# Recurrent stage with its factors two units ahead, its gated outputs spread over the next units, and the prompt's operands asked for at its end

## The chip, the cores and the metric

The kernel runs on one core of one Trainium2 chip. The metric is device time in microseconds (us) of one execution: 2415.64 us, the median of 3 runs (2414.82 to 2417.95). The engines are TensorE (PE; its weight loads are PEld), VectorE (DVE), ScalarE (ACT), GpSimd (POOL) and SyncE (SP), whose queue issues nearly all loads and stores (SPq).

## The reference

One inference step of a hybrid layer for a prompt of 2048 tokens and 8 samples of 4 tokens. One RMSNorm and one combined input projection (1024 to 5912 columns) feed two branches:

- native sparse attention: compressed, top-8 selected and window branches over 8 heads, with gates;
- HGRN2, a gated linear recurrence, 4 heads of 128 by 128 state;

both are gated, projected, merged through sigmoid gates (ma, mb), projected once more, added to the input and normalised. The recurrence is the part at issue:

```python
def step(S, xs):
    qc, kc, vc, gc = xs
    G = jnp.cumsum(gc, axis=2)
    o_inter = jnp.einsum('bhtd,bhde->bhte', qc * jnp.exp(G), S)
    D = jnp.where(tri, G[:, :, :, None, :] - G[:, :, None, :, :], -jnp.inf)
    A = jnp.einsum('bhtd,bhtsd,bhsd->bhts', qc, jnp.exp(D), kc)
    o = o_inter + jnp.einsum('bhts,bhse->bhte', A, vc)
    S = jnp.exp(Gl)[..., None] * S + jnp.einsum('bhsd,bhse->bhde', kc * jnp.exp(Gl[:, :, None, :] - G), vc)
...
o = o * lax.rsqrt(jnp.mean(o * o, axis=-1, keepdims=True) + EPS)
return o.reshape(B, T, B_WIDTH) * norm_g * jax.nn.silu(zB), S
```

## The kernel before

The kernel is one program whose stages are written as Python generators. `along(steps, ns)` runs a stage: after each `yield` it calls `fill(ns)`, which emits input projection matmuls worth about ns nanoseconds. A projection matmul multiplies float16 pairs (high and low parts), three products of 8 by 128x128 for each block of up to 512 tokens: 24 matmuls into one accumulator `ps` (two of them, `fps`). The groups of columns come in a fixed order (q, f, qb, ib, zb, z, ma, mb); the last, mb ("gate", L424), goes in pieces of 512 or 272 tokens, each through ScalarE into one of 3 buffers (`row`, later `piece`) and by a store (mb_d, L441) to memory.

The code gives only a priority. A scheduler puts every engine's instructions into one fixed order, by this priority and by its own estimate of what is ready. The engines then run their orders strictly, waiting on one another by semaphores.

The recurrent stage, `hgrn()` (L620), handles **units**: a chunk of 256 tokens and one of 4 heads, 32 units in all; the four heads of a chunk are a **group** here. Of a unit:

- `factors` loads the unit's operands and makes the decayed factors: a scan G and the subtractions on VectorE (five X, L728), exponentials on ScalarE, products on GpSimd (L731, L732, L693 to L703).
- `scores` transposes Kd (L739) and makes the two 128x128 score blocks out of small matmuls (L751, L755); VectorE masks them into AT (own, L762 to L765).
- `values` multiplies with v and with the state S (pu L774, ov L778 and L780), updates S on VectorE (L785), and ScalarE copies o and sums its squares into `ss` (L790, L793).

One unit's factors are made while the unit before goes through `values`. After the fourth head of a chunk, `rsqrt` makes the reciprocal root by a Newton chain of 16 small VectorE instructions (L649, L237 to L244, L651), and `gate_out` is emitted for the four heads in a row: VectorE scales o (L656), TensorE transposes it (L659), VectorE multiplies by zt (L662), and the halves gh, gl are stored to obh_d, obl_d. Beside the units, from the seventh on, `sample_heads` handles the 4 heads of the samples step by step; its state update multiplies kd with v masked for 4 samples at a time (vm on VectorE, L836; product L838).

Behind the stage comes `attention_setup` (it loads szs and stores oah_d, oal_d, L1409 to L1414), then `prompt_phase`: `open_block` loads the queries of the first blocks (L1500 to L1503), `want` the window keys (L1480 to L1485), `load_keys` the rest (L1359 to L1365); `prep` makes the compressed scores (L1567 to L1607) of two blocks with `pfill` between its steps; then the attention runs block by block, with what is left of the mb pieces and the output projections (L1777) between its tiles.

Of the kernel before, what the change touches and what calls it, by code (L numbers as in the profile page):

```python
# [10 lines left out]
F32 = mybir.dt.float32  # L11
F32R = mybir.dt.float32r
F16 = mybir.dt.float16
# [8 lines left out]
NP = 2048  # L22
# [109 lines left out]
def trunk_kernel(ctx: ExitStack, tc: tile.TileContext, A, O):  # L132
# [487 lines left out]
    def hgrn():  # L620
        with ExitStack() as st:
# [4 lines left out]
            lmf = hc.tile([128, 8, 32], F32, name="lmf")  # L626
            sy.dma_start(lmf, A["c_lmask"].rearrange("p (l t) -> p l t", l=8))
            lmi = hc.tile([128, 8, 32], I32, name="lmi")
            ve.tensor_copy(lmi, lmf)
# [17 lines left out]
            def rsqrt(ss):  # L647
                n = ss.shape[0]
                ve.tensor_scalar(ss, ss, 1.0 / 128, EPS, op0=OP.mult, op1=OP.add)  # L649
                y = newton_rsqrt(ss, hp)  # L650
                ve.tensor_scalar(y, y, sob[:n], None, op0=OP.mult)  # L651
                return y

            def gate_out(o_sb, zt, y, nt, r, h, t0):

                ve.tensor_tensor(o_sb[:r, :nt], o_sb[:r, :nt], y[:r, :nt, None].to_broadcast([r, nt, 128]), op=OP.mult)  # L656
                pt = po.tile([128, 512], F32, name="ov")
# [12 lines left out]
            def common(h, t0, n, L):  # L670
# [24 lines left out]
                Xo = new("Xo")  # L695
# [5 lines left out]
                Kd = new("Kd", bufs=1)  # L701
                ac.activation(Kd, E2, AF.Exp)
                gp.tensor_mul(Kd, Kd, kt)  # L703
                eG = hp.tile([128, 8], F32, name="eG" + sfx)[:, :n // L]
# [10 lines left out]
            def factors(c, h):  # L715
                t0 = c * NC
                G, qt, kt, Bq, Bk, Xo, Kd, eG = common(h, t0, NC, 128)
                v = hp.tile([128, NJ, 128], F32, name="v")
# [17 lines left out]
            def scores(u):  # L736
# [6 lines left out]
                for j in range(NJ):  # L743
# [18 lines left out]
                    ve.tensor_mul(own, near[:, 3], lmf[:, 3])  # L762
# [7 lines left out]
            def values(u, ss):  # L770
# [20 lines left out]
                for j in range(NJ):  # L791
                    jk = hp.tile([128, 128], BF, name="jk")
                    ac.activation(jk, ov[:, j], AF.Square, accum_out=ss[:, h * NJ + j:h * NJ + j + 1])  # L793
# [4 lines left out]
            def sample_heads():  # L798
                for h in range(4):
# [4 lines left out]
                    sy.dma_start(S0, A["state_hgrn"][0, :, h].rearrange("b d e -> d b e"))  # L804
                    pb = po.tile([128, 512], F32, name="pk")
                    mm(pb[:32, :32], Bk, Bq, True, True)
                    AT = hp.tile([32, 32], F32, name="ATs")
                    ve.tensor_mul(AT, pb[:32, :32], lmf[:32, 3])
# [13 lines left out]
                    jk = hp.tile([32, 128], BF, name="jk_s")  # L822
                    ac.activation(jk, pt[:32, :128], AF.Square, accum_out=ss)
                    y = rsqrt(ss)
                    yield
                    gate_out(o_sb, load_z(h, 2048, 32), y, 1, 32, h, 2048)
                    pk = po.tile([128, 512], F32, name="pk").rearrange("p (a b) -> p a b", a=4)
                    pe.transpose(pk[:32, 0], Kd, ident)
                    kd = hp.tile([32, 128], F32, name="kd_s")
# [3 lines left out]
                    for b2 in range(2):  # L833
                        vm = hp.tile([32, 4, 128], F32, name="vm", bufs=1)
                        for b in range(4):
                            ve.tensor_scalar(vm[:, b], v, bd[:, 4 * b2 + b:4 * b2 + b + 1], None, op0=OP.mult)  # L836
                        pu = po.tile([128, 512], F32, name="pu").rearrange("p (a b) -> p a b", a=4)
                        mm(pu, kd, vm, True, True)  # L838
                        for b in range(4):
                            bb = 4 * b2 + b  # L840
                            ve.scalar_tensor_tensor(Sn[:, bb], S0[:, bb], eG[:, bb:bb + 1], pu[:, b], op0=OP.mult, op1=OP.add)
                    sy.dma_start(O["s_hgrn"][0, :, h].rearrange("b d e -> d b e"), Sn)

            beside = sample_heads()
            units = [(c, h) for c in range(NP // NC) for h in range(4)]
            ahead = [factors(*units[0])]
            yield
            yield from scores(ahead[0])
            outs = []
            for k, (c, h) in enumerate(units):  # L850
# [3 lines left out]
                u = ahead.pop(0)  # L854
                if k + 1 < len(units):
                    ahead.append(factors(*units[k + 1]))
                    yield
                    yield from scores(ahead[0])
# [7 lines left out]
                if h == 3:  # L866
                    y = rsqrt(ss)
                    for h2 in range(4):
                        gate_out(*outs[h2], y[:, h2 * NJ:(h2 + 1) * NJ], NJ, 128, h2, c * NC)
                        yield  # L870
# [476 lines left out]
    def attention_setup(st, a):  # L1347

        pc_ = st.enter_context(tc.tile_pool(name="pc", bufs=1, side="right"))
        KA, KB, V = a["KA"], a["KB"], a["V"]  # L1350
        a["sel0"] = pc_.tile([128, 16, 32], F32, name="h_sel0")
        for g in range(2):
            KA["s", g] = pc_.tile([100, NP], F16, name=f"kas{g}")
            KB["s", g] = pc_.tile([128, NP], F16, name=f"kbs{g}")
        V["s"] = pc_.tile([128, 16, 2, 129], F16, name="vs16")

        def load_keys(t0, t1):
            if t0 == 0:
                sy.dma_start(a["sel0"], A["c_sel0"].rearrange("p (t j) -> p t j", j=32))  # L1359
# [60 lines left out]
    def prompt_phase(a, st, pfill, state, sw):  # L1420
        KA, KB, V, TB, TQ = a["KA"], a["KB"], a["V"], a["TB"], a["TQ"]
        pu = st.enter_context(tc.tile_pool(name="pu", bufs=2, side="right"))
        pst = st.enter_context(tc.tile_pool(name="pst", bufs=2, space=PSUM, side="right"))
        pmx = st.enter_context(tc.tile_pool(name="pmx", bufs=3, space=PSUM, side="right"))
# [197 lines left out]

        state["env"]["tp"] = lambda: pmx.tile([128, 4, 128], F32, name="mx").rearrange("p a b -> p (a b)")
        wc = sw.enter_context(tc.tile_pool(name="wc", bufs=3))
        state["env"]["piece"] = lambda: wc.tile([128, 512], F32, name="piece")
        for i in range(2):
            open_block(i)
            if i == 0:
                want(ORDER[0])
                a["load_keys"](0, 512)  # L1630
            else:
                a["load_keys"](512, NP)
# [346 lines left out]
        return main  # L1979

    with ExitStack() as s2:
# [22 lines left out]
        along(hgrn(), 1250.0)  # L2004
        fill(0, ("z", 2))
        fill(350.0)
        along(attention_setup(s2, att), 15000.0)
        fill(0, ("ma", 6))
        sb.close()
        prompt_phase(att, s2, fill, state, sw)()  # L2010
# [31 lines left out]
```

## Time and profile before

| what | value |
|---|---|
| median of 3 runs | 2415.64 us |
| profiled execution | 2413.94 us |
| its span | 2412.2 us |
| mean granted TensorE clock | 0.98 |
| TensorE busy | 2279.5 us, 94% |
| VectorE busy | 1533.5 us, 64% |
| ScalarE / GpSimd busy | 1182.3 us / 1021.4 us |
| recurrent stage, first transposes to last gated product | 638 to 1323 us |

TensorE's busy time is the sum of stretches in which a matmul is recorded; what it lacks to the span are gaps. A clock under 1.00 in a stretch says that for a part of it the granted clock was the lower of its two levels (1.2 instead of 2.4 GHz). An idle time in brackets names the instruction that ended the wait.

### The profile page before, as it was taken

Reading aid. Unit: us, or ns where it says so; the run is one execution under the profiler, and the core shown is the slowest. Engines: PE = TensorE matmul, PEld = TensorE weight load, DVE = VectorE, ACT = ScalarE, POOL = GpSimd, SP = SyncE. Lnnn points to the kernel's source line nnn. Section 1 sums busy time; section 2 is a strip of 40 time slices with the busy share of each in tenths; the row PEclk is TensorE's granted clock in tenths of the full one; section 3 lists DMA queues with packets and bytes.
Section 4 is the critical chain, followed back from the end, with each engine's and each line's share of the span. In section 5 each row is a group of like instructions: output and inputs, shape, how many; then the busy total and the mean of one; then the engine's idle time right before and its main releaser. Section 6 shows DMA issues by size and latency. Waiting matters only on the chain.

```text
span 2412.2 us, 56868 instructions
## 1 busy us (share of the span) xinstructions
PE 2279.5 (94%) x22181; PEld 1545.1 (64%) x22181; DVE 1533.5 (64%) x4088; ACT 1182.3 (49%) x2606; POOL 1021.4 (42%) x1184
## 2 busy tenths in 40 slices
PE   6999998999899998999989799899999999999998
PEld 5898775555685555556656456667677666665765
DVE  7555554756613689777774356768677677767543
ACT  5544332521422266555663256356556566667663
POOL 0000102242500056555550035356656567777764
PEclk9999999999999999999999899999999999999999
DMA  6643313676842443333332533432222221211121
GB/s 205 178 127 117 127 71 107 230 257 219 256 125 75 152 142 112 115 111 116 117 102 93 141 121 95 111 85 80 63 85 83 61 63 43 72 50 48 52 58 43
DMA packets 276109, 271.89 MB, mean 113 GB/s; under 512 B 102296, under 2 KB 246176, under 8 KB 268416
## 3 DMA queue, kind: packets, MB, share of 16 engines
q1 hardware_dynamic: 267328, 230.51, 31.2%
q0 software_dynamic: 8512, 37.75, 4.7%
q8 instruction: 174, 2.85, 0.5%
q14 instruction: 95, 0.78, 0.1%
HBM read 184.66 MB, written 87.74 MB: 113 GB/s over the span
## 4 chain that ended last, share of the span: by engine, by line
PE 72%; DVE 11%; DMA 6%; ACT 4%; issue 3%; SPq 2%; POOL 1%; ACTq 0%; POOLq 0%; DVEq 0%
PE ps L375 17%; PE ps L1809 7%; PE ps L1777 7%; PE ps L456 7%; PE ps L435 5%; PE st L1666 3%; PE st L1656 3%; PE mx L1536 3%; PE ph L969 2%; DVE X L728 2%; PE po L1461 2%; PE po L1462 2%; PE po L1464 2%; DMA wraw<-in_w_in_dram 1%; PE pt L952 1%
## 5 line engine op out<-in xcount | busy, mean ns | idle before, releaser
L1455 POOL TENSOR_TENSOR Pl<-P,Ph 128x512 f16<-128x512 f32 x444 | 522.1, 1186 | 316.6 <-ACT Ph L1454 178.6
L1453 ACT ACTIVATE P<-st 128x512 f32<-128x512 f32 x444 | 264.8, 597 | 239.8 <-PE st L1666 185.3
L375 PEld LDWEIGHTS <-wh 128*128 128x128 f16 x2240 | 216.0, 98 | 167.8 <-issue 16.2
L1454 ACT ACTIVATE Ph<-st 128x512 f16<-128x512 f32 x444 | 263.1, 595 | 10.5 <-PE po L1462 8.3
L375 PE MATMUL ps<-xh,wh 128*128 128x512 f16 (+1 forms) x1120 | 229.6, 342 | 4.7 <-DVE row L388 3.5
L375 PE MATMUL ps<-xh,wl 128*128 128x512 f16 (+1 forms) x1120 | 232.9, 343 | 0.0
L375 PE MATMUL ps<-xl,wh 128*128 128x512 f16 (+1 forms) x1120 | 231.7, 341 | 0.5 <-issue 0.5
L1539 DVE TENSOR_REDUCE mps<-mx 128x1 f32<-128x512 f32 (+3 forms) x320 | 185.8, 602 | 60.3 <-PE mx L1538 29.5
L456 PE MATMUL ps<-wh,xh 128*128 128x256 f16 (+1 forms) x680 | 190.3, 280 | 10.1 <-ACT to L464 4.8
L456 PE MATMUL ps<-wh,xl 128*128 128x256 f16 (+1 forms) x680 | 189.2, 279 | 4.1 <-DVE xl L341 4.1
L456 PE MATMUL ps<-wl,xh 128*128 128x256 f16 (+1 forms) x680 | 189.9, 279 | 0.0
L1461 PEld LDWEIGHTS <-Ph 128*128 128x128 f16 x1776 | 139.8, 98 | 39.5 <-ACT Ph L1454 5.2
L375 PEld LDWEIGHTS <-wl 128*128 128x128 f16 x1120 | 109.4, 99 | 83.1 <-issue 6.1
L456 PEld LDWEIGHTS <-xh 128*128 128x128 f16 x1360 | 131.1, 99 | 32.4 <-issue 7.7
L1462 PEld LDWEIGHTS <-Ph 128*128 128x128 f16 x1776 | 128.4, 97 | 32.6 <-issue 0.5
L697 POOL TENSOR_TENSOR Xo<-Xo,qt 128x256 f32<-128x256 f32 x32 | 33.3, 1041 | 260.7 <-ACT Xo L696 210.0
L1539 DVE TENSOR_REDUCE mpw<-mx 128x1 f32<-128x512 f32 (+3 forms) x224 | 102.8, 482 | 40.5 <-PE mx L1538 40.0
L1777 PEld LDWEIGHTS <-xh 128*128 128x128 f16 x1280 | 105.0, 98 | 32.7 <-issue 7.1
L731 POOL TENSOR_TENSOR X<-X,kt 128x128 f32<-128x128 f32 x160 | 91.5, 574 | 65.4 <-ACT X L730 63.0
L1464 PEld LDWEIGHTS <-Pl 128*128 128x128 f16 x1776 | 94.2, 97 | 25.9 <-POOL Pl L1455 8.8
L1461 PE MATMUL po<-vs,Ph 128*128 128x65 f16 x1088 | 105.5, 192 | 2.6 <-DVE otmp L1553 2.0
L1462 PE MATMUL po<-vs,Ph 128*128 128x64 f16 x1088 | 104.8, 193 | 0.0
(528 smaller groups left out, 5824.0 us busy)
## 6 DMA issues: line engine op xcount, KB each, us to landing
wraw<-in_w_in_dram SPq DMA_DIRECT2D x22, 1024.0 KB
xt<-in_x_prompt_dram SPq DMA_DIRECT2D x32, 512.0 KB
ma_d<-row SPq DMA_DIRECT2D x8, 1040.0 KB
out_y_prompt_dram<-xt SPq DMA_DIRECT2D x16, 512.0 KB
sg<-ma_d SPq DMA_DIRECT2D x56, 128.0 KB
sg<-mb_d SPq DMA_DIRECT2D x56, 128.0 KB
q_d<-row SPq DMA_DIRECT2D x4, 1040.0 KB
lf_d<-row SPq DMA_DIRECT2D x4, 1040.0 KB
```

The source lines that it names most:

```text
L375: mm(ps, l[:, kc], xs(r, t0, n)[:, kc], k == 0, k == 23)
L435: mm(ps, l[:, kc, a * 128:(a + 1) * 128], xs(r, t0, n)[:, kc], k == 0, k == 23)
L456: mm(ps, x, w[:, kc], k == 0, k == 23)
L1453: ac.activation(P[:n], ps, AF.Exp, scale=1.0 / QS)
L1454: ac.activation(ph[:n], ps, AF.Exp, scale=1.0 / QS)
L1455: sub.tensor_sub(pl[:n], P[:n], ph[:n])
L1461: mm(po[:, r, :w], ph[:n, rs[r]], v[:n, :w], first and r == 0, False)
L1462: mm(po[:, r, :64], ph[:n, rs[r]], v[:n, w:w + 64], False, False)
L1464: mm(po[:, r, :w], pl[:n, rs[r]], v[:n, :w], False, last)
L1539: ve.tensor_reduce(mp_[:, r, c:c + 1], pmf[:, :n], axis=AX.X, op=OP.max)
L1777: mm(X["ps"], w[:, kc, cs], os_[o][:, kc], k == 0, k == 11)
L1809: mm(X["ps"], X["y"][y][:, kc, i0:i0 + r], W["o", kc // 4][w][:, kc % 4, cs], k == 0, k == 23)
```

## The change

1. `factors` runs two units ahead, not one; Kd, v, Xo and eG get one more buffer, jk one less, and the mask constant is loaded into a borrowed tile, of which only a 32-column part is kept (lm3).
2. Scaling (`gate_scale`) is split off `gate_out`. The four gated outputs of a chunk wait in a list `ready`; each of the next four units asks for one scale at its start and emits one `gate_out` before its values.
3. `sample_heads` makes its masks (`masked`) a step ahead of the product that reads them, and takes one step more a head.
4. `fill` after a step of the stage is asked for 1200, not 1250 ns.
5. `prompt_phase` is a generator too. Its first part, the loads of block 0 and its window keys, is emitted at the end of the recurrent stage, before `attention_setup`; the tiles of the keys are made later, in `load_keys`.

```diff
@@ -623,10 +623,12 @@
...
-            lmf = hc.tile([128, 8, 32], F32, name="lmf")
-            sy.dma_start(lmf, A["c_lmask"].rearrange("p (l t) -> p l t", l=8))
+            lm = hp.tile([128, 256], F32, name="X0").rearrange("p (l t) -> p l t", l=8)
+            sy.dma_start(lm, A["c_lmask"].rearrange("p (l t) -> p l t", l=8))
...
-            ve.tensor_copy(lmi, lmf)
+            ve.tensor_copy(lmi, lm)
+            lm3 = hc.tile([128, 32], F32, name="lm3")
+            ve.tensor_copy(lm3, lm[:, 3])
@@ -647,13 +649,15 @@
...
-                y = newton_rsqrt(ss, hp)
-                ve.tensor_scalar(y, y, sob[:n], None, op0=OP.mult)
+                y = hp.tile([128, 8], F32, name="rsy", bufs=3)[:n, :ss.shape[1]]
+                ve.tensor_scalar(y, newton_rsqrt(ss, hp), sob[:n], None, op0=OP.mult)
...
-            def gate_out(o_sb, zt, y, nt, r, h, t0):
+            def gate_scale(o_sb, y, nt, r):
...
+
+            def gate_out(o_sb, zt, nt, r, h, t0):
@@ -692,16 +696,16 @@
...
-                Xo = new("Xo")
+                Xo = new("Xo", bufs=3)
...
-                Kd = new("Kd", bufs=1)
+                Kd = new("Kd")
...
-                eG = hp.tile([128, 8], F32, name="eG" + sfx)[:, :n // L]
+                eG = hp.tile([128, 8], F32, name="eG" + sfx, bufs=3)[:, :n // L]
@@ -715,7 +719,7 @@
...
-                v = hp.tile([128, NJ, 128], F32, name="v")
+                v = hp.tile([128, NJ, 128], F32, name="v", bufs=3)
@@ -759,7 +763,7 @@
...
-                    ve.tensor_mul(own, near[:, 3], lmf[:, 3])
+                    ve.tensor_mul(own, near[:, 3], lm3)
@@ -789,7 +793,7 @@
...
-                    jk = hp.tile([128, 128], BF, name="jk")
+                    jk = hp.tile([128, 128], BF, name="jk", bufs=1)
@@ -802,10 +806,17 @@
...
+                    vm = hp.tile([32, 4, 128], F32, name="vm", bufs=1)
+
+                    def masked(b2):
+                        for b in range(4):
+                            ve.tensor_scalar(vm[:, b], v, bd[:, 4 * b2 + b:4 * b2 + b + 1], None, op0=OP.mult)
+
+                    masked(0)
...
-                    ve.tensor_mul(AT, pb[:32, :32], lmf[:32, 3])
+                    ve.tensor_mul(AT, pb[:32, :32], lm3[:32])
@@ -819,43 +830,64 @@
...
-                    jk = hp.tile([32, 128], BF, name="jk_s")
+                    jk = hp.tile([128, 128], BF, name="jk", bufs=1)[:32]
...
-                    y = rsqrt(ss)
+                    gate_scale(o_sb, rsqrt(ss), 1, 32)
...
-                    gate_out(o_sb, load_z(h, 2048, 32), y, 1, 32, h, 2048)
+                    gate_out(o_sb, load_z(h, 2048, 32), 1, 32, h, 2048)
...
-                    kd = hp.tile([32, 128], F32, name="kd_s")
+                    kd = hp.tile([32, 128], F32, name="kd_s", bufs=1)
...
-                        vm = hp.tile([32, 4, 128], F32, name="vm", bufs=1)
-                        for b in range(4):
-                            ve.tensor_scalar(vm[:, b], v, bd[:, 4 * b2 + b:4 * b2 + b + 1], None, op0=OP.mult)
...
+                        if b2 == 0:
+                            masked(1)
...
+                        if b2 == 0:
+                            yield
...
+
...
+            for _ in range(3):
+                yield
+            ahead.append(factors(*units[1]))
...
-            outs = []
+            outs, ready = [], []
+
+            def gated(step):
+
+                if ready:
+                    o_sb, zt, y, h2, c2 = ready[0]
+                    if step == 0:
+                        gate_scale(o_sb, y, NJ, 128)
+                    else:
+                        gate_out(o_sb, zt, NJ, 128, h2, c2 * NC)
+                        ready.pop(0)
+
...
+                gated(0)
+                if k + 2 < len(units):
+                    ahead.append(factors(*units[k + 2]))
+                    yield
...
-                    ahead.append(factors(*units[k + 1]))
+                    yield from scores(ahead[0])
+                if ready:
+                    gated(1)
...
-                    yield from scores(ahead[0])
@@ -865,9 +897,13 @@
...
-                    for h2 in range(4):
-                        gate_out(*outs[h2], y[:, h2 * NJ:(h2 + 1) * NJ], NJ, 128, h2, c * NC)
-                        yield
+                    ready = [(*outs[h2], y[:, h2 * NJ:(h2 + 1) * NJ], h2, c) for h2 in range(4)]
+            while ready:
+                gated(0)
+                yield
+                next(beside, None)
+                gated(1)
+                yield
@@ -1346,16 +1382,16 @@
...
-        pc_ = st.enter_context(tc.tile_pool(name="pc", bufs=1, side="right"))
...
-        a["sel0"] = pc_.tile([128, 16, 32], F32, name="h_sel0")
-        for g in range(2):
-            KA["s", g] = pc_.tile([100, NP], F16, name=f"kas{g}")
-            KB["s", g] = pc_.tile([128, NP], F16, name=f"kbs{g}")
-        V["s"] = pc_.tile([128, 16, 2, 129], F16, name="vs16")
...
+                pc_ = st.enter_context(tc.tile_pool(name="pc", bufs=1, side="right"))
+                a["sel0"] = pc_.tile([128, 16, 32], F32, name="h_sel0")
+                for g in range(2):
+                    KA["s", g] = pc_.tile([100, NP], F16, name=f"kas{g}")
+                    KB["s", g] = pc_.tile([128, NP], F16, name=f"kbs{g}")
+                V["s"] = pc_.tile([128, 16, 2, 129], F16, name="vs16")
@@ -1420,8 +1456,6 @@
...
-        pst = st.enter_context(tc.tile_pool(name="pst", bufs=2, space=PSUM, side="right"))
-        pmx = st.enter_context(tc.tile_pool(name="pmx", bufs=3, space=PSUM, side="right"))
@@ -1620,15 +1654,19 @@
...
+        open_block(0)
+        want(ORDER[0])
+        yield
+        pst = st.enter_context(tc.tile_pool(name="pst", bufs=2, space=PSUM, side="right"))
+        pmx = st.enter_context(tc.tile_pool(name="pmx", bufs=3, space=PSUM, side="right"))
...
-            open_block(i)
...
-                want(ORDER[0])
...
+                open_block(1)
@@ -1976,7 +2014,7 @@
...
-        return main
+        main()
@@ -2001,13 +2039,16 @@
...
-        along(hgrn(), 1250.0)
+        along(hgrn(), 1200.0)
...
+        prompt = prompt_phase(att, s2, fill, state, sw)
+        next(prompt)
...
-        prompt_phase(att, s2, fill, state, sw)()
+        for _ in prompt:
+            pass
...

```

The scheduler turns this into new orders on all engines. Three places follow, before and after.

VectorE, first group of four units, from the start of the Newton chain (ss is the sum of squares, rsq and rsz are the chain's values). Before:

```order
L649 TENSOR_SCALAR ss<-ss 128x8
L237 TENSOR_SCALAR rsq<-ss 128x8
L685 SCALAR_TENSOR_TENSOR G<-rst,lf 128x256
L238 TENSOR_TENSOR rsq<-magic,rsq 128x8
L688 TENSOR_TENSOR E<-G 128x256
L700 TENSOR_TENSOR E<-G 128x256
L241 TENSOR_TENSOR rsz<-rsq 128x8
L242 TENSOR_TENSOR rsz<-rsz,ss 128x8
L243 TENSOR_SCALAR rsz<-rsz 128x8
L244 TENSOR_TENSOR rsq<-rsq,rsz 128x8
```

After:

```order
L651 TENSOR_SCALAR ss<-ss 128x8
L692 TENSOR_TENSOR E<-G 128x256
L237 TENSOR_SCALAR rsq<-ss 128x8
L732 TENSOR_TENSOR X_9881<-G 128x256
L732 TENSOR_TENSOR X_9887<-G 128x256
L732 TENSOR_TENSOR X_9893<-G 128x256
L766 TENSOR_TENSOR own<-p_9724,lm_8646 128x32
L238 TENSOR_TENSOR rsq<-magic,rsq 128x8
L732 TENSOR_TENSOR X_9899<-G 128x256
L732 TENSOR_TENSOR X_9905<-G 128x256
L766 TENSOR_TENSOR own<-p_9759,lm_8646 128x32
```

The chain's rows stood nearly next to each other; now the X and own rows of later units stand between them.

SyncE, end of the recurrent stage: gh and gl are its last gated output, szs and OSh, OSl belong to `attention_setup`, qs, qc, qb are the queries of block 0. Before:

```order
L667 DMA obh_d<-gh 128x256
L668 DMA obl_d<-gl 128x256
L441 DMA mb_d<-piece 128x272
L1409 DMA szs<-sz_d 64x8x32
L1359 DMA h_sel_16055<-in_c_sel_dram 128x512
L1361 DMA kas_16056<-ksx_d_89 64x512
L1362 DMA kbs_16057<-ksx_d_89 128x512
L1364 DMA kas_16056<-in_c_kblk_dram 36x2048
L1413 DMA oah_d<-OSh 64x8x32
L1414 DMA oal_d<-OSl 64x8x32
L1361 DMA kas_16058<-ksx_d_90 64x512
L1362 DMA kbs_16059<-ksx_d_90 128x512
```

After:

```order
L671 DMA obh_d<-gh 128x256
L672 DMA obl_d<-gl 128x256
L441 DMA mb_d<-row 128x272
L1534 DMA qs<-qh_d 64x4x128
L1534 DMA qc<-qh_d 64x4x128
L1534 DMA qb<-qh_d 64x4x128
L1535 DMA qc<-tc_d_87 32x512
L1537 DMA qb<-ql_d 64x4x128
L1534 DMA qs<-qh_d 64x4x128
L1534 DMA qc<-qh_d 64x4x128
L1534 DMA qb<-qh_d 64x4x128
L1535 DMA qc<-tc_d_88 32x512
```

The loads of block 0 stood behind szs and the stores of OSh and OSl; now they follow the last store of the recurrent stage, and szs stands behind all 24 of them and three stores of pieces.

TensorE, first two blocks of the prompt's preparation: xd carries the maxima, st are compressed scores, Ph their probabilities, ps and wh a piece of the mb projection. Before:

```order
L1445 MATMUL mx<-h_id,xd_16447 128x128
L1576 LDWEIGHTS kac_6516
L1576 MATMUL st<-qc,kac_6516 128x512
L1576 LDWEIGHTS kac_6525
L1576 MATMUL st<-qc,kac_6525 128x512
L1461 LDWEIGHTS Ph
L1461 MATMUL mx<-vc,Ph 128x97
L1462 LDWEIGHTS Ph
```

After:

```order
L435 MATMUL ps<-xh_124,wh 128x272
L1610 LDWEIGHTS kac_6516
L1610 MATMUL st<-qc,kac_6516 128x512
L435 LDWEIGHTS wh
L435 MATMUL ps<-xl_128,wh 128x272
L1610 LDWEIGHTS kac_6525
L1610 MATMUL st<-qc,kac_6525 128x512
L435 LDWEIGHTS wh
```

Between the second score product and the first probability product stood nothing; now 27 projection matmuls follow the second score product before the first probability product, and one stands between the two.

## Rows read from the trace of the kernel before

**Rows 1.** The page's busy line: us, share of the span, instructions.

```profile
PE 2279.5 (94%) x22181; PEld 1545.1 (64%) x22181; DVE 1533.5 (64%) x4088; ACT 1182.3 (49%) x2606; POOL 1021.4 (42%) x1184
```

**Rows 2.** Stretches: length, busy us of PE, PEld, DVE, ACT, POOL, clock, DMA.

```profile
864.00:990.00 126.00, 115.38 (x1240) 72.54 (x1239) 113.33 (x316) 78.88 (x266) 80.45 (x130) 0.96 0.37 122
990.00:1294.00 304.00, 287.32 (x2919) 181.50 (x2916) 214.87 (x657) 166.90 (x577) 146.82 (x246) 0.98 0.34 108
1294.00:1324.00 30.00, 30.00 (x152) 14.99 (x150) 14.95 (x57) 8.17 (x15) 0.00 (x0) 1.00 0.31 100
1324.00:1400.00 76.00, 62.29 (x391) 35.01 (x390) 29.49 (x101) 17.41 (x27) 5.45 (x9) 0.87 0.50 141
1500.00:1600.00 100.00, 89.56 (x1069) 64.44 (x1067) 74.42 (x252) 46.67 (x92) 47.56 (x56) 0.95 0.41 108
900.00:950.00 50.00, 42.56 (x515) 27.92 (x514) 47.00 (x147) 30.46 (x110) 35.09 (x58) 0.90 0.30 93
1150.00:1200.00 50.00, 48.29 (x564) 31.79 (x563) 39.08 (x118) 33.43 (x116) 29.74 (x47) 1.00 0.43 137
```

**Rows 3.** TensorE in order of time, recurrent stage: start, us, what [idle before].

```profile
935.11 0.66 PE L659 MATMUL ov<-ident,o_sb 128*128 128x128 f32 x2 [4.94 <-DVE o_sb L656]
...
985.73 1.09 PE L838 MATMUL pu<-vm,kd_s 32*128 32x512 f32 x2 [2.29 <-DVE own L764]
...
1051.68 1.09 PE L838 MATMUL pu<-vm,kd_s 32*128 32x512 f32 x2 [3.42 <-DVE vm L836]
...
1264.61 0.69 PE L659 MATMUL ov<-ident,o_sb 128*128 128x128 f32 x2 [4.99 <-DVE o_sb L656]
```

**Rows 4.** Chain of waits, 1290 to 1420: start, us, what.

```profile
1326.88 2.47 DMA szs<-sz_d
...
1331.06 2.24 DMA oal_d<-OSl
1333.36 0.60 SPq L1500
...
1349.47 3.45 DMA mb_d<-piece
...
1371.61 1.17 POOL Pl L1455
...
1404.38 5.18 PE ps L435 x24
```

**Rows 5.** TensorE in order of time, prompt's preparation and first output product.

```profile
1353.75 1.87 PE L435 MATMUL ps<-xh,wh 128*128 128x512 f16 x4 [3.35 <-ACT piece L440]
...
1379.37 0.45 PE L1603 MATMUL mx<-ident,repp 128*128 128x128 f32 x1 [2.68 <-DVE repp L1599]
...
1519.03 0.47 PE L1603 MATMUL mx<-ident,repp 128*128 128x128 f32 x1 [3.12 <-DVE repp L1599]
1522.42 0.27 PE L1777 MATMUL ps<-oah,xh 128*128 128x32 f16 x4 [2.92 <-DMA oah<-oah_d]
```

**Rows 6.** VectorE in order of time, second group: start and scaling of the chain.

```profile
926.60 0.43 DVE L649 TENSOR_SCALAR ss<-ss 128x8 f32<-128x8 f32 x1
...
934.54 0.76 DVE L656 TENSOR_TENSOR o_sb<-o_sb,rsq 128x256 f32<-128x256 f32 x2
```

**Rows 7.** TensorE in order of time, start of the recurrent stage.

```profile
638.27 0.44 PE L739 MATMUL pk<-ident,Kd 128*128 128x128 f32 x2 [3.08 <-POOL Kd L703]
...
642.20 0.69 PE L751 MATMUL p<-X 128*64 128x64 f32 x4 [3.49 <-POOL X L732]
...
851.56 0.62 PE L780 MATMUL ov<-S,Xo 128*128 128x128 f32 x2 [2.26 <-DVE S L783]
```

**Rows 8.** Tile X, 870 to 1290: ns min/median/max, first and last start.

```profile
L728 DVE TENSOR_TENSOR X<-G x125: 396/417/959, 873.8 to 1257.6; 128x256 f32<-128x256 f32 x125
...
L731 POOL TENSOR_TENSOR X<-X,kt x125: 442/458/2510, 878.7 to 1263.4; 128x128 f32<-128x128 f32 x125
```

**Rows 9.** Groups by line, VectorE, 864 to 1294: busy us, mean ns, idle.

```profile
L728 DVE TENSOR_TENSOR X<-G 128x256 f32<-128x256 f32 x125 | 68.6, 603 | 0.0
```

## The prediction

> **What bounds the kernel now.** I read the page's busy line first, then stretches, then the waits inside them, then the chain of waits. TensorE is busy 94% of the span [rows 1], so only two things can shorten it: gaps between its matmuls and half-clock time. The stretches [rows 2] show where these are. I count as lost, in each, the time without matmuls plus (1 − granted clock) × length.
>
> - 864 to 990, the middle of the recurrent stage (units 4 to 11, from unit 3's state update to unit 11's): 10.6 + 5.0 = 15.7 us lost, VectorE busy 113.3 of 126 us, 90%.
> - 990 to 1294 (units 12 to 31): 16.7 + 6.1 = 22.8 lost, VectorE 71%.
> - 1294 to 1324, the stage's tail: nothing.
> - 1324 to 1400, the prompt phase's preparation: 13.7 + 9.9 = 23.6 lost.
> - 1500 to 1600: 10.4 + 5 = 15.4 lost.
>
> The waits behind these numbers [rows 3]: twice some 5 us for a gated product whose scaling VectorE had not done (935, 1264), 3.4 and 2.3 us at the sample update. At 1324 to 1354 the chain [rows 4] leaves the engines for SyncE's queue: the sample's szs load, its store behind VectorE, then the loads of block 0 one by one from 1333 on, and behind them the store of a finished gate piece, without which ScalarE had no buffer and TensorE stood 3.35 us [rows 5]. Then come the short steps of the preparation with nothing between them, up to the 2.68 us at 1379.
>
> **The change, part by part.** Work on TensorE is the same, but for where projection matmuls stand. I count them in sets of 24 of 512 columns; one takes 5.18 us [rows 4].
>
> *Less projection inside the stage.* From unit 3 to 11 there were 14.1 sets, now 12.9 (6.4 us less); from 11 to 31 37.7, now 31.5 (32.3 us less). They are run later, so this gains nothing: the same stretches with the loss they have now, but the new sets, would take 126 − 6.4 = 119.6 and 304 − 32.3 = 271.7 us. Free of loss they are 103.9 and 248.9.
>
> *VectorE does not shrink with them.* Between the same state updates it has 312 instructions before and 308 now, then 657 and 652 (two of the 2 us weight passes fewer, about 5 us). So it needs 113 us where TensorE needs 104, and 210 where TensorE needs 249. In units 4 to 11 VectorE is the bound: at its 90% of today they take 126 us, a loss of 22 where it is 15.7; at 97%, 117 us, a loss of 13. The first is as likely as the second, so I take 17. For units 12 to 31 VectorE's share rises from 71% to about 82%. Spreading removes the places where its work came in a heap, so the loss may fall to 7 us (2 to 3%), or stay at 8%, 20 us. I take 13. Together 30 against 38.5: 8 us gained, between 4 us lost and 18 gained.
>
> *Gated outputs, one per unit.* The scale is asked for a unit ahead, but the order shows that all four scales still stand together behind the reciprocal root. What moved is the root's chain: between its first row and the scales stood 27, 29, 29, 27, 25, 26, 35, 16 rows in the eight groups, now 45, 37, 34, 51, 37, 49, 31, 16. The first product stands about as far behind its unit as before (9 to 12 us of matmuls, now 9.5 to 14). In the second group the chain took 926.6 to 934.5, 8 us, and TensorE waited 4.94 [rows 3, 6]. So I count the first product of a group as a wait that stays and only the second to fourth as free; this is in the 17 and 13.
>
> *Masks a step ahead.* At 1051 the sample's second update product waited 3.42 us for its masks, at 985 the first 2.29 us. With the masks made a step earlier both waits, 5.7 us [rows 3], should go; they are part of the 8 us.
>
> *Two units ahead, at the start.* The projection matmuls in front of the first transposes are the same, so the 3.08 and 3.49 us at 638 and 642 and the 2.26 at 851 [rows 7] stay: 0. The further buffers, the moved mask constant and the shared scratch tile cost one small VectorE copy, under 1 us, early in the stage, where the clock and TensorE wait for loads.
>
> *Prompt operands at the stage's end.* The 24 loads stand now in front of szs and its stores. They still wait for the stage's last store, since they take its memory. At 0.6 us each [rows 4] they hold SyncE 14 us, and the piece stores behind them wait so long. TensorE has 5.7 sets, 29 us, between the last gated product and the first compressed logits (it had 3.0, 15.5 us). Three piece buffers and two accumulators hold some 21 us of them (two pieces of 272 columns, three of 512); the queue is free again after 14 us and a landing before and behind of 2.2 us each, as the store of the chain took, 19 in all: the 3.35 us should go, with little to spare. The preparation now has 2 to 6 us of projection between its steps, against links of up to 1.17 us [rows 4], so most of its waits go; the last selection step still has none (2.68 us stays). Of 23.6 us lost I keep 8: 15 to 16 gained, at least 0, at most 20.
>
> *Block 0's first output product* at 1519 [rows 5]: the selection wait (3.12) and the load (2.92) have the same neighbours now. I take 0, with 4 us either way.
>
> The sum against the profiled execution, 2413.9 us (span 2412.2 and 1.7 around it): 8 + 15.5 = 24 us less, 2390. The median shown is 1.7 above that execution, so **2392**. Its own range is 2380 to 2404, the middle part of both terms' ends (2 to 16 and 10 to 20 us gained).
>
> **A rule that speaks against it.** The subtraction that makes X on VectorE reads two operands in SBUF and takes 396 ns at the least and 959 at the most; GpSimd's product beside it takes 442 to 2510 [rows 8]. The Trainium skill (SBUF — State Buffer, "Who interferes with whom") says that a VectorE instruction with two SBUF inputs and a GpSimd instruction that reads SBUF take turns at one port pair, the later one blocked for the whole instruction. The spread in the rows agrees with that, and by the rule a stage in which both are denser would slow both. It is the last rival.
>
> **Rivals.**
> 1. *The recurrent waits go altogether.* With factors two units ahead VectorE could run at 97% in units 4 to 11, and the products of a group could all come after their scales: loss 13 + 4, so 21 us gained, and 20 at the boundary: 2374. For it: 1150 to 1200 lost only 1.7 us with VectorE at 78% [rows 2]. Against it: VectorE needs more than TensorE in units 4 to 11.
> 2. *The boundary keeps its wait.* SyncE's block is only moved ahead; if the release comes later or the loads take longer, the gate pieces run out of buffers at another place and the preparation is late. Gain 4 to 8 in the stage, 0 here: 2410.
> 3. *Slower: the root's chain sets the pace.* The eight chains have 300 rows instead of 214; 86 rows at VectorE's 0.35 us (328 us for 973 rows, [rows 2]) are 30 us, and the product waits for each if VectorE is full. After the wait of 4.94 us the granted clock was 0.90 over 900 to 950 [rows 2], its lower level for a part: 5 us more; three such add 15. Less masks 6 and boundary 15: 24 us slower, 2440. It decides once each of the seven long chains costs over 3 us more wait.
> 4. *Slower by the port.* If each of 125 subtractions took the longest 959 ns instead of the mean 603 [rows 8, 9], VectorE would need 45 us more; 372 us at 90% are 414 for both stretches, where 391 holds today's loss: 23 slower, less 15: 2424.
>
> **Chances.** Forecast 0.50, rival 1 0.20, rival 2 0.16, rival 3 0.09, rival 4 0.05. The range reaches from just under rival 1 to rival 2 and the near part of rivals 3 and 4: 2372 to 2420. A difference within 0.2% (4.8 us) can't be told from none. The forecast is faster but for 0.02 beyond its own range, rival 1 wholly, rival 2 in 0.07 of its 0.16, else the same; rivals 3 and 4 are slower but for 0.02: faster 0.75, same 0.13, slower 0.12.
>
> **What would show it.** Right: units 4 to 11 with VectorE at 90% or more and TensorE's loss still near 17; no sample-update wait over 1 us; the first product of a group waiting more than the other three; the chain at the stage's end without SyncE, no wait for a piece, and one selection wait near 3 us. Wrong: the boundary's 24 us still lost, or half-clock stretches at most groups. My sum fails if the recurrent stage gains over 20 us or loses any.

## The result and the profile after

The changed kernel takes 2393.57 us (median of 4 runs, 2388.3 to 2394.5), the kernel before beside it 2416.8 (4 runs): ratio 0.9891, 95% interval 0.9871 to 0.9911. That is 23 us faster by the medians and 26 by the ratio. A second measurement, on a later occasion, gave 0.9904 (0.9890 to 0.9918). The profiled execution has a span of 2392.4 us against 2412.2.

The busy line of the page answers to [rows 1]; below it are stretches between the same points of the program as in [rows 2] (length, then busy us of PE, PEld, DVE, ACT and POOL, clock, DMA share, GB/s):

```profile
PE 2276.5 (95%) x22181; PEld 1543.9 (65%) x22181; DVE 1523.3 (64%) x4089; ACT 1180.8 (49%) x2606; POOL 1018.8 (43%) x1184
```

```profile
865.00:984.00 119.00, 110.31 (x1164) 69.78 (x1162) 112.33 (x313) 77.00 (x263) 78.64 (x129) 0.94 0.39 125
984.00:1250.00 266.00, 257.67 (x2773) 163.38 (x2774) 198.17 (x657) 159.80 (x573) 146.69 (x245) 0.99 0.36 113
...
1274.00:1304.00 30.00, 30.00 (x173) 16.82 (x172) 7.99 (x35) 6.63 (x9) 0.82 (x5) 1.00 0.43 115
1304.00:1404.00 100.00, 94.64 (x691) 54.48 (x690) 46.54 (x132) 35.78 (x57) 18.54 (x16) 0.97 0.45 132
1404.00:1504.00 100.00, 90.22 (x985) 62.63 (x984) 63.69 (x204) 60.15 (x103) 48.55 (x48) 0.96 0.40 112
1504.00:1604.00 100.00, 95.81 (x1138) 67.58 (x1137) 73.99 (x242) 46.08 (x96) 49.56 (x57) 0.99 0.33 87
```

Units 4 to 11 are the first row, 12 to 31 the second, the first compressed logits come at 1304. The recurrent units take 385 us instead of 430, and lose 8.7 + 7.1 = 16 and 8.3 + 2.7 = 11 us; before it was 15.7 and 22.8. VectorE is busy 94% of the first row, 74% of the second. Behind 1304 the first 100 us lose 9 us; before, the first 100 us behind the first logits (at 1339) lost 24.

TensorE's longest waits there, singly (start, us, what, idle before and what ended it), answer to [rows 3, 5]:

```profile
927.55 0.40 PE L822 MATMUL pu<-ATs,vs__10316 32*128 32x32 f32 x2 [3.03 <-DVE S L789]
...
998.71 0.69 PE L663 MATMUL ov<-ident,o_sb 128*128 128x128 f32 x2 [3.41 <-DVE o_sb L658]
...
1110.61 0.44 PE L663 MATMUL ov<-ident,o_sb 128*128 128x128 f32 x2 [1.99 <-DVE o_sb L658]
...
1356.10 0.45 PE L1637 MATMUL mx<-ident,repp 128*128 128x128 f32 x1 [3.29 <-DVE repp L1633]
...
1499.27 0.48 PE L1637 MATMUL mx<-ident,repp 128*128 128x128 f32 x1 [5.26 <-DVE repp L1633]
```

The waits for masks are gone; those for a scaled output fell from 10.7 to 5.7 us, the two long ones each the first of its group. The new wait at 927 is one of VectorE's own order. VectorE in order of time there:

```profile
924.38 0.50 DVE L397 SCALAR_TENSOR_TENSOR row<-ps,neg,row 128x272 f32<-128x272 f32 x1
924.92 2.32 DVE L207 TENSOR_REDUCE trk<-row 128x1 f32<-128x2080 f32 x1
927.16 0.34 DVE L789 SCALAR_TENSOR_TENSOR S<-S,eG,pu 128x128 f32<-128x128 f32 x1
```

A state update of 0.34 us, for which TensorE waits, stands behind a maximum of 2.32 us that it does not need. The chain of waits at the stage's end (start, us, what) answers to [rows 4]:

```profile
1277.80 0.38 POOL xd L1467 x2
1278.18 0.13 SPq L1534
1278.36 0.62 SPq L1534
...
1292.54 0.43 SPq L1519
1293.07 0.41 SPq L441
...
1294.51 2.61 DMA szs<-sz_d
...
1298.81 0.59 SPq L1450
1299.45 0.63 SPq L1534
```

The loads of block 0 run behind GpSimd's release of their memory from 1278 to 1293, then the piece stores, then szs. The chain still goes through SyncE, but TensorE has no gap from 1274 to 1304.

### The profile page after: what moved, and what is told of

Same layout as the page of the kernel before. It is cut to its first block, busy times and chain, and to the rows that moved or that the text cites. A ratio compares the mean times of both kernels' runs of the same rounds, so it can differ in the third digit from the quotient of the medians.

```text
span 2392.4 us, 56947 instructions
## 1 busy us (share of the span) xinstructions
PE 2276.5 (95%) x22181; PEld 1543.9 (65%) x22181; DVE 1523.3 (64%) x4089; ACT 1180.8 (49%) x2606; POOL 1018.8 (43%) x1184
## 4 chain that ended last, share of the span: by engine, by line
PE 75%; DVE 9%; DMA 6%; ACT 3%; issue 3%; SPq 2%; POOL 1%; another core or an unknown queue 0%; DVEq 0%; POOLq 0%; ACTq 0%
PE ps L375 19%; PE ps L1847 7%; PE ps L1815 7%; PE ps L456 6%; PE ps L435 5%; PE st L1704 3%; PE st L1694 3%; PE mx L1570 3%; PE ph L1005 2%; PE po L1495 2%; PE po L1498 2%; PE po L1496 2%; PE pt L988 1%; DMA wraw<-in_w_in_dram 1%; PE mx L1572 1%
## 5 line engine op out<-in xcount | busy, mean ns | idle before, releaser
L375 PE MATMUL ps<-xh,wh 128*128 128x512 f16 (+1 forms) x1120 | 234.4, 344 | 6.2 <-DVE row L388 3.5
L1847 PE MATMUL ps<-xh,yh 128*128 128x512 f16 (+1 forms) x272 | 103.0, 379 | 2.3 <-DVE pr L1818 2.3
```

What stands on the lines that cost most here:

```text
L375: mm(ps, l[:, kc], xs(r, t0, n)[:, kc], k == 0, k == 23)
L1847: mm(X["ps"], X["y"][y][:, kc, i0:i0 + r], W["o", kc // 4][w][:, kc % 4, cs], k == 0, k == 23)
```

## The experiments

Two counts describe the runs. *Sets* are the prediction's (24 matmuls of 512 columns, 5.18 us), taken from the program order: those from unit 3's values to the last gated product, and those left behind the first compressed logits. *Lost* is the time without matmuls plus half of the time at the lower clock, between the state updates of units 3 and 31, and in the 300 us behind the first logits.

| kernel | sets, units 4 to 31 | sets left | lost, units 4 to 31 | lost, 300 us | ratio to before (95%) |
|---|---|---|---|---|---|
| before | 57.7 | 15.2 | 39 | 40 | 1 |
| changed | 49.6 | 20.1 | 27 | 28 | 0.9891 (0.9871 to 0.9911) |
| changed, again (e10) | 49.6 | 20.1 | 27 | 28 | 0.9904 (0.9890 to 0.9918) |
| prompt part alone (e1) | 57.7 | 16.6 | 40 | 41 | 0.9989 (0.9976 to 1.0002) |
| recurrent part alone (e2) | 49.6 | 18.5 | 30 | 28 | 0.9923 (0.9908 to 0.9938) |
| the same, again (e11) | 49.6 | 18.5 | 27 | 30 | 0.9923 (0.9908 to 0.9938) |
| outputs at once (e4) | 58.2 | 15.4 | 26 | 53 | 0.9988 (0.9977 to 0.9999) |
| one unit ahead (e5) | 49.7 | 23.4 | 29 | 34 | 0.9959 (0.9944 to 0.9973) |
| masks late (e6) | 49.6 | 20.1 | 26 | 32 | 0.9913 (0.9896 to 0.9930) |
| less filler (e9) | 49.6 | 14.7 | 28 | 33 | 0.9860 (0.9846 to 0.9874) |
| outputs later (e3) | 49.5 | 22.4 | 22 | 27 | 0.9858 (0.9839 to 0.9877) |
| the same, again (e12) | 49.5 | 22.4 | 26 | 22 | 0.9865 (0.9850 to 0.9879) |
| later, 1100 (e7) | 45.6 | 26.0 | 32 | 28 | 0.9879 (0.9861 to 0.9898) |
| later, 1000 (e8) | 42.2 | 32.5 | 38 | 31 | 0.9921 (0.9908 to 0.9935) |

e1 to e4 ran on one chip, e5 to e8 on a second, e9 to e12 on a third, each with before beside them.

Three more counts come from the same traces. *Rest* is the length of units 4 to 31, between the same state updates, less 5.18 us for each set that runs there. The *preparation* is the stretch from the first compressed logits to the fourth selection product (`repp`), the last of its two blocks; its sets stand between its steps.

| count | before | e1 | e5 | changed | e4 | e6 | e9 | e2, e11 | e3, e12 | e7, e8 |
|---|---|---|---|---|---|---|---|---|---|---|
| rest, us | 161 | 162 | 161 | 153 | 154 | 153 | 154 | 155, 152 | 142, 146 | 150, 164 |
| sets in the preparation | 3.0 | 4.4 | 11.0 | 7.9 | 3.1 | 7.9 | 6.5 | 6.2, 6.2 | 10.1, 10.1 | 10.6, 13.2 |
| lost in the preparation, us | 21 | 19 | 8 | 5 | 25 | 7 | 10 | 5, 5 | 8, 5 | 2, 1 |

The preparation in before, the changed kernel, e4 and e9:

```profile
1339.00:1380.00 41.00, 27.56 (x170) 13.33 (x168) 13.87 (x68) 9.44 (x16) 4.62 (x4) 0.80 0.57 156
```

```profile
1304.00:1356.00 52.00, 47.47 (x330) 27.45 (x328) 15.84 (x68) 12.90 (x22) 4.62 (x4) 1.00 0.60 169
```

```profile
1316.00:1360.00 44.00, 29.30 (x174) 14.06 (x172) 16.13 (x71) 9.61 (x16) 4.62 (x4) 0.77 0.58 151
```

```profile
1305.00:1355.00 50.00, 42.09 (x297) 24.85 (x294) 16.30 (x69) 12.80 (x22) 4.62 (x4) 0.95 0.61 172
```

**The two parts by themselves.** e1 is the kernel before with the prompt part of the diff, e2 the kernel before with all of the diff but that.

```diff
# e1
...
-        along(attention_setup(s2, att), 15000.0)
+        prompt = prompt_phase(att, s2, fill, state, sw)
+        next(prompt)
+        along(attention_setup(s2, att), 15000.0)
...
# e2: the diff's hunks inside hgrn, and
-        along(hgrn(), 1250.0)
+        along(hgrn(), 1200.0)
```

> The kernel before with the prompt part alone (block 0's loads and first window asked for at the recurrent stage's end, the pools opened behind them); the recurrent stage stays as it was, 3.0 sets of projection matmuls in its tail. Theory A (the sum's second term): the loads leave the chain, the preparation has projection between its steps, 15 to 16 us less, about 2401, ratio 0.9936, and its stretch loses some 8 us instead of 23.6. Theory B (the release comes too late, the first rival at this place): nothing gained, 2417. Theory C: the loads need the longer tail (5.7 sets) that the other part gives; with 3.0 sets half the loss stays, 6 to 9 us gained, about 2409.

> The recurrent part alone (two units ahead, gated outputs spread, masks early, the share of projection of the changed kernel), the prompt part as before. Theory A: 8 us less in the stage, the boundary's 23.6 us stay, about 2409, ratio 0.9967; both parts together then add up to the 23 us of the whole change. Theory C: the longer tail by itself already takes part of the boundary's loss, 14 to 18 us less, about 2401.

The prompt part alone brings 0.1%, not distinguishable from nothing. TensorE's waits there, 1300 to 1420 (us in total, times, longest):

```profile
PE mx L1459 <- ACT Ph L1452: 3.9, 2, 3.3
PE mx L1601 <- DVE repp L1597: 2.7, 1, 2.7
PE st L1573 <- DMA qb<-ql_d: 2.2, 1, 2.2
```

The wait for a piece is gone as forecast. In its place TensorE waits for links of the preparation, and 2.2 us for a load of block 0 (qb). The recurrent part alone brings 0.8%, and with the loads as late as before it loses no more at the boundary than the whole change. First 100 us behind the first logits, e1, then e2's kernel in its second run (e11):

```profile
1318.00:1418.00 100.00, 87.07 (x645) 48.16 (x644) 45.97 (x135) 36.36 (x57) 18.79 (x17) 0.91 0.45 130
```

```profile
1314.00:1414.00 100.00, 94.84 (x726) 55.52 (x725) 47.58 (x145) 37.95 (x61) 21.29 (x19) 0.97 0.34 103
```

12.9 us without matmuls and a clock of 0.91 against 5.2 and 0.97. So A does not hold, and B has the number of e1 but not its reason, since the wait for a piece is gone. The boundary's gain comes with the recurrent part. Theory C pointed to the longer tail; it has e2 right (18 us less), not e1 (3 us instead of 6 to 9). The next runs show what is behind it.

**Spreading.** In e4 a group's four outputs are scaled and emitted at its end again.

```diff
-                    ready = [(*outs[h2], y[:, h2 * NJ:(h2 + 1) * NJ], h2, c) for h2 in range(4)]
+                    for h2 in range(4):
+                        gate_scale(outs[h2][0], y[:, h2 * NJ:(h2 + 1) * NJ], NJ, 128)
+                        gate_out(*outs[h2], NJ, 128, h2, c * NC)
+                        yield
```

> The changed kernel with the four gated outputs of a group made at once at its end, as before the change; factors two units ahead and early masks stay. If spreading them gives the stage's gain: two waits of some 5 us come back, each with 3.4 us of half clock behind it, 10 to 17 us more, 2403 to 2410. If the gain comes from the factors and masks: no more than 4 us slower, up to 2397.

Nearly all is lost (0.9988), more than the 10 to 17 us expected, and not by the waits that I expected. Units 4 to 11 and 12 to 31, then the first 100 us behind the first logits:

```profile
853.00:974.00 121.00, 112.77 (x1266) 71.77 (x1264) 113.01 (x312) 79.09 (x269) 75.82 (x126) 0.97 0.38 124
974.00:1279.00 305.00, 299.03 (x2906) 186.81 (x2905) 205.03 (x665) 165.91 (x572) 143.22 (x246) 0.97 0.34 109
...
1316.00:1416.00 100.00, 82.24 (x623) 44.42 (x621) 51.26 (x167) 38.62 (x63) 25.36 (x23) 0.86 0.44 125
```

In the units TensorE loses no more than in the changed kernel (26 us), yet they take 41 us longer: 58.2 sets of projection stand in them, 8.6 more. Both kernels ask for seven steps a unit at 1200 ns, 28 units: 235 us, 45 sets. The scheduler puts in more, 13 sets with the outputs at once, 4 with them spread; presumably where its estimate finds no recurrent step ready, which no run shows. These are sets that the preparation then lacks: its first 100 us lose 31 us, with three waits for the selection:

```profile
PE mx L1640 <- DVE repp L1636: 9.2, 3, 4.8
PE mx L1482 <- DVE xd L1479: 2.3, 2, 2.1
PE mx L1498 <- ACT Ph L1491: 1.6, 3, 0.7
```

The kernel before, with as few sets left, loses 24 in its first 100 us; why it is 31 here stays open. The rest of the units stays at 154 us, so what the stage itself gains does not come from the spreading.

**Taking filler away.** If the sets left over are the gain, taking them away must cost nearly the time that they take.

```diff
+                last = 15 if c0 >= 5400 else 23
-                for l, r in ((wh, "h"), (wh, "l"), (wl, "h")):
+                for l, r in ((wh, "h"), (wh, "l"), (wl, "h"))[:(last + 1) // 8]:
...
-                        mm(ps, l[:, kc, a * 128:(a + 1) * 128], xs(r, t0, n)[:, kc], k == 0, k == 23)
+                        mm(ps, l[:, kc, a * 128:(a + 1) * 128], xs(r, t0, n)[:, kc], k == 0, k == last)
```

> The changed kernel without the third of the three products (low part of the weights) in the last two groups of gate columns: 5.4 sets, 28 us of matmuls (5.18 us a set), are left out, so its gates are less exact. The program order is the same up to the first compressed logits; 14.7 sets are left behind them instead of 20.1 (before: 15.2). Filler theory (what is left behind the stage fills the preparation's waits, and that is the boundary's gain): of the 28 us only 14 to 18 are saved, the 300 us behind the first logits lose about 40 us again (27.9 in the changed kernel, 40.4 before); ratio to before 0.981 to 0.984. If the early loads are what covers the preparation: all 28 us saved, loss there near 28; ratio 0.977 to 0.979.

> The changed kernel once more, on the chip of the next two: ratio 0.987 to 0.991, 15 to 16 us of the loss before gone at the boundary, 12 in units 4 to 31. It is the base for both.

28 us of matmuls fewer save 11.8 us (2378.86 against 2390.65), less than either theory expected. Stretches behind the first logits of the kernel with less filler, then of the changed kernel on the same chip:

```profile
1305.00:1405.00 100.00, 91.66 (x691) 54.39 (x688) 51.59 (x136) 43.08 (x66) 20.65 (x17) 0.95 0.53 158
1405.00:1505.00 100.00, 88.54 (x1090) 60.64 (x1089) 64.66 (x240) 59.99 (x114) 51.91 (x58) 0.97 0.40 109
```

```profile
1303.00:1403.00 100.00, 93.84 (x686) 53.84 (x685) 46.48 (x132) 35.81 (x57) 19.65 (x17) 0.98 0.42 129
1403.00:1503.00 100.00, 90.40 (x1009) 63.11 (x1008) 64.39 (x209) 61.47 (x105) 48.42 (x48) 0.96 0.41 114
```

Of the 16 us that are missing, 9 are lost in the 600 us behind the first logits (33 + 3 against 28 + 0), 3.7 in the first 600 us of the profiled executions, where both programs are the same, and 5 in the last 100 us (18.5 against 13.6), far behind the sets. So the 28 us of sets were worth some 9 us where they ran. The 33 us are fewer than the 40 expected: 5 come back in the preparation, and the loss is spread wider, up to the output products, which now wait 3.2 us once for a load of oal. The theory of the loads, with all 28 saved, is out.

**The parts of the recurrent change.** e5 takes one lead back, e6 the early masks.

```diff
# e5
-            for _ in range(3):
-                yield
-            ahead.append(factors(*units[1]))
...
-                if k + 2 < len(units):
-                    ahead.append(factors(*units[k + 2]))
+                if k + 1 < len(units):
+                    ahead.append(factors(*units[k + 1]))
...
-                if k + 1 < len(units):
...
# e6
-                    masked(0)
...
+                        masked(b2)
                         mm(pu, kd, vm, True, True)
-                        if b2 == 0:
-                            masked(1)
```

> The changed kernel with factors made one unit ahead again; spread outputs, early masks, the share of 1200 and the prompt part stay. In its program order units 4 to 31 take 49.7 sets of projection (the changed kernel 49.6, before 57.7) and 23.4 sets are left behind the first compressed logits (20.1, before 15.2). If what counts is how much projection the stage uses up as filler (filler theory): as fast as the changed kernel within 5 us, ratio 0.987 to 0.991, since the spread alone holds the sets back. If the factors' lead is what lets TensorE run on: at least half of the whole gain is lost, ratio 0.994 or more.

> The changed kernel with the samples' masks made right before the products that read them, as before; sets in the stage and left behind it as in the changed kernel (49.6 and 20.1). Prediction's term: waits of 3.4 and 2.3 us for masks come back, up to 6 us more, ratio 0.990 to 0.9935. Rival: VectorE reaches the masks in time once the outputs are spread: no difference, ratio 0.988 to 0.990.

One unit ahead costs over half of the gain, though the sets are held back and 23.4 are left: here the count of sets alone foretold wrongly. Units 4 to 31 take 392 us against 384 with the same sets, and their rest is 161 us, as before the change. So the lead is what the stage gains by: e4 and e6, which keep it, keep the 8 us. Only 2 of them show as loss, the others as longer stretches in which some matmul is recorded.

The boundary of e5 loses 6 us more than that of the changed kernel, with more sets left, and 8 us are lost in its first 20. Three piece stores stand behind the loads of block 0 in SyncE's queue, ScalarE waits for a buffer, and TensorE for ScalarE:

```profile
1294.64 2.62 SPq L441 DMA_DIRECT2D mb_d<-row  x3
...
1298.27 0.49 ACT L440 ACTIVATE row<-ps,neg 128x272 f32<-128x272 f32 x1 [2.99 <-DMA mb_d<-row]
...
1298.81 3.57 PE L435 MATMUL ps<-xh,wh 128*128 128x512 f16 x8 [3.10 <-ACT row L440]
```

Sets are no cover while their buffers are held. The late masks cost nothing that the intervals tell from the changed kernel (0.9913 against 0.9891 and 0.9904), and no wait for a mask is in the trace: with the rest of the recurrent change VectorE is there in time anyway.

**Outputs one unit later, and the share.** Here a group's first scale is asked for a unit later still.

```diff
+                go = h or len(ready) > 4
-                gated(0)
+                if go:
+                    gated(0)
...
-                if ready:
+                if ready and go:
...
-                    ready = [(*outs[h2], ...) for h2 in range(4)]
+                    ready += [(*outs[h2], ...) for h2 in range(4)]
# e7 also:
-        along(hgrn(), 1200.0)
+        along(hgrn(), 1100.0)
# e8: 1000.0
```

> The changed kernel with each group's gated outputs one unit later, so that its root chain has a whole further unit (some 14 us) before the first scale. If the first products wait for the root chain: the waits of 3.41 us (995) and 1.99 us (1108) and the 3.4 us of half clock behind the first go, units 12 to 31 lose 3 us instead of 11, about 2385 (2383 to 2388). If VectorE's queue as a whole is the cause, another of its instructions is waited for in their place: within 3 us of the changed kernel, 2391 to 2396.

> The changed kernel with each group's gated outputs one unit later, on the same chip: 5 to 9 us faster than the changed kernel, ratio 0.984 to 0.987, with no first product of a prompt group waiting; if the difference of the first look (0.9858 to 0.9891) came from the chip: within 3 us of it.

On one chip 0.9865 against 0.9904: 9 us faster than the changed kernel, and the fastest full kernel here. TensorE's waits in units 4 to 31 of e12, and of the changed kernel, the longest groups:

```profile
PE ov L782 <- DVE zt L666: 3.7, 2, 1.9
PE ps L375 <- DVE row L397: 3.0, 1, 3.0
```

```profile
PE ov L663 <- DVE o_sb L658: 5.7, 3, 3.4
PE pu L822 <- DVE S L789: 3.0, 1, 3.0
```

No wait for o_sb is left, so the first product did wait for its scale, and a unit more is enough. But the loss of units 12 to 31 did not fall to 3 us as expected (10 in e3, 14 in e12): the gain stands in the rest of units 4 to 31, 142 and 146 us instead of 153, and at the boundary.

> The changed kernel with each group's gated outputs one unit later and 1100 instead of 1200 ns of projection asked for after a step: 45.6 sets in units 4 to 31 (with 1200: 49.5) and 26.0 left behind the first compressed logits (22.4). Filler theory: the four sets are worth more in the preparation: of the 27 us lost in the 300 us behind the first logits 5 to 10 go, the stage loses 0 to 5 more: ratio 0.982 to 0.986 (0.9858 with 1200). If VectorE's share of the stage decides: the stage loses the 20 us that the sets no longer cover, ratio 0.990 or more.

> As the last, with 1000 ns: 42.2 sets in units 4 to 31, 32.5 left behind the first compressed logits. Units 4 to 11 have 11.2 sets, fewer than the 12.3 beside which VectorE was the bound already. Filler theory: the preparation can't lose less than its own chains, so what the stage loses now outweighs: 3 to 15 us slower than with 1100, ratio 0.984 to 0.992. If the stage has room left: ratio 0.979 to 0.983.

Fewer sets in the units (45.6, 42.2) cost there 32 and 38 us lost, and the boundary gains nothing more (28, 31), where 5 to 10 us were expected of e7: its preparation loses only 2 and 1 us, but the third 100 us lose 21 and 24. More sets left than in e3 and e12 (22.4) bring nothing there, and they are missing beside VectorE, which is busy 99.6 of 107 us (e7) and 99.9 of 107 us (e8) in units 4 to 11.

**The prompt part beside the recurrent one.** e11 is e2's kernel on the chip of e10.

> The recurrent part alone on the same chip as the changed kernel. The prompt part alone was worth 0.1% (0.9989), so by the filler theory it is worth little beside the recurrent part too: 0 to 5 us slower than the changed kernel, ratio 0.988 to 0.992. If the early loads matter once TensorE has projection to go on with: 6 to 12 us slower, ratio 0.993 or more.

0.9923 against 0.9904: 5 us, with intervals that overlap. Together with e1 the prompt part is worth 0 to 5 us.

## Why the prediction was right, and where it was wrong

The time (2392 forecast, 2393.57 measured) and the sum hold: 24 us forecast, 20 between the two profiled spans (of the second, the first 600 us, which the change does not touch, lost 4.6 us more), 23 and 26 by the ratios.

- *Units 4 to 11:* VectorE at 90 to 97% and 17 us lost were forecast; 94% and 16 came. *Units 12 to 31:* 13 forecast, 11 measured, but VectorE was busy 198 us (74%), not 210 (82%). The stage's term of 8 us measured 12 as loss and 8 as rest (161 to 153 us), inside its bounds.
- *The reason of that term was wrong.* I put it on the spreading and the masks, and the second unit ahead had no term but a 0 at the stage's start. e4 and e6 take spreading and early masks back and keep the 8 us; e5 takes the lead back and loses them.
- *Gated outputs:* the first of a group waits, the others do not, as said; e3 and e12 show that the scale is the cause.
- *Masks:* the waits of 5.7 us went, but the step that was credited for it is not the cause: e6 has the masks late and no such wait.
- *Less projection inside the stage: "They are run later, so this gains nothing".* This step failed. The sets that the units no longer take are cover for the boundary: with 3 to 4.4 of them between its steps the preparation loses 19 to 25 us, with 6 and more 10 at most, and 28 us of sets are worth some 9 (e9). Their number is not all: e2 loses 5 us with 6.2, e9 10 with 6.5.
- *Prompt operands at the stage's end:* the term has the right size (8 us lost between 1274 and 1380, 8 forecast) and in the main a wrong cause. I named the sets between the steps, but took them as given and booked what they bring under the early loads. The piece wait does go with the loads, but alone they bring 2.6 us (e1, up to 5.8), and without them the boundary is as good (e2, e11). So it is in part luck that the time came out: two terms had the right size for other reasons than those given. The sign "chain without SyncE" was wrong, and it didn't matter.
- *Block 0's first product:* 0 with 4 us either way; 1480 to 1580 lost 19 us instead of 15.4, a selection wait of 5.26 us.
- *Rival 1* (2374) asked for outputs that all come after their scales: that is e12's kernel, not this one. *Rival 2* (2410) has the boundary of e1, where nothing is gained; its pieces that run out of buffers at another place are seen in e5. *Rival 3:* the root chains are longer in rows, but waits for scales fell to 5.7 us. *Rival 4:* X got faster, though VectorE and GpSimd are both busier. By line, units 4 to 11 before, then the same and units 12 to 31 in the changed kernel (622 ns before):

```profile
L728 DVE TENSOR_TENSOR X<-G 128x256 f32<-128x256 f32 x40 | 20.7, 564 | 0.0
```

```profile
L732 DVE TENSOR_TENSOR X<-G 128x256 f32<-128x256 f32 x40 | 18.9, 511 | 1.0 <-PE p L755 0.9
...
L732 DVE TENSOR_TENSOR X<-G 128x256 f32<-128x256 f32 x85 | 36.7, 476 | 0.8 <-PE p L755 0.7
```

## What to carry to other kernels

Work that depends on nothing is a store of cover: count how much of it each stage takes up beyond what was asked for, and what the next stage with long chains then has left. A stage that takes less of it can shorten a later one, without an edit there, as long as the work finds its buffers free. When two edits are made at once, the place of the gain does not name its cause; one run with each alone does. Gaps and clock do not show all that a stage loses: compare also its length less its known work.

## What the hardware showed that was not expected

The kernel before took 2416.8, 2404.1, 2417.6 and 2412.5 us on four occasions. The stretch from 400 to 500 us, the same program in before and in e1, first before, then e1:

```profile
400.00:500.00 100.00, 91.31 (x699) 53.06 (x700) 59.48 (x120) 44.66 (x52) 37.88 (x36) 0.97 0.64 220
```

```profile
400.00:500.00 100.00, 98.68 (x802) 58.82 (x800) 63.78 (x136) 50.15 (x58) 46.48 (x45) 1.00 0.71 249
```

In the second execution transfers ran at 249 GB/s and TensorE was busy 98.7%, in the first 220 and 91.3%; over the first 600 us 37 us were lost against 52.5. The four traces of that occasion (e1 to e4) lost 37 to 42 us there, the ten others 51 to 59. Whether it is the chip, these runs don't show. That is more than most edits here are worth, so spans of different occasions are not compared above, only ratios and losses of stretches.
